# Batched inverses in smaller bundles, another accumulator bank for a transposing stage, and an undivided last tile

## The chip, the cores and the metric

The kernel runs on one core of one Trainium2 chip. The core has a matmul engine (PE, with its weight loads PEld), a vector engine (DVE), an activation engine (ACT), a small general engine (POOL) and a queue that issues transfers (SP). The metric is the device time of one execution in microseconds; smaller is better. The kernel before was run three times: 1584.83, 1586.66 and 1587.31 us.

## The reference

One layer of a decoder on 1024 tokens of width 2048, all in float32. A normalised input is projected, three groups of heads work on the columns, and a second projection with a residual and a final norm closes it.

```python
h = rmsnorm(x, ln_g[l])
proj = h @ w_in[l]
# group A: per chunk of 128 tokens, four groups of 128 channels
out_a = gmlp_spatial_gating(g_u, g_v, ...) * silu(g_z)
# group B: 8 heads of 128, chunks of 64 tokens
a = where(strict, einsum('bhnid,bhnjd->bhnij', kb, k) * decay, 0.0)
T = triangular_solve(a + eye, eye, left_side=True, lower=True, unit_diagonal=True)
value = einsum('bhnij,bhnjd->bhnid', T, vb)
...
_, o = lax.scan(step, s0, xs)          # state from chunk to chunk
out_b = rmsnorm(o, dn_norm_g[l]) * silu(d_z)
# group C: attention into 256 memory tokens, 4 heads
out_c = softmax(scores) @ mv * silu(c_z)
x = x + concatenate([out_a, out_b, out_c]) @ w_out[l]
return rmsnorm(x, final_g)
```

The spatial gating normalises `gelu(g_v)` over its 512 channels and multiplies it, chunk by chunk, by a lower triangular 128x128 matrix per group.

## The kernel before

**Tiling.** Both projections are cut into two halves of tokens, two halves of the inner dimension and two halves of columns, and are computed with seven products of half-size blocks in place of eight (`seven`, L1289; the order of the seven is `ORDER`). Every float32 operand is split into a rounded part and a remainder (`split_to`: a cast on ACT, a subtraction on DVE), and each product is the sum of three matmuls of 128x128 by 128x512, so almost all of PE's time is 128x512 matmuls into eight accumulator banks: `acc0` to `acc3` and `dn0` to `dn3` (in the profile `acc` and `dn`). In the order listings below the numbers behind the names are those of the buffers: `dn_111` to `dn_114` are `dn0` to `dn3`, `acc_107` to `acc_110` are `acc0` to `acc3`.

**Stages.** The projection runs as `project_stage` calls: columns of the first four delta heads, of the other four, gates and values, then pairs of column blocks for groups A and C, then the output projection. The small work of the heads runs between the large matmuls: `front` (convolution, norms and the chunk matrices of a pair of heads), `inverse` and `levels` (the triangular inverses of 32 chunk matrices at once, called twice: "a" for heads 0 to 3, L1550, and "b" for heads 4 to 7, L1646), `back` (the scan over chunks), `spatial` (the normalisation of `g_v`, L1620), `attend`.

**The inverses.** `inverse` inverts the 32x32 diagonal blocks on DVE, and `levels` (L1032) joins them to 64x64 and then 128x128 blocks with small float32 products on PE, in the banks `dn0` and `dn1` (there called `da`, `db`, and `dy` for both). Each batch of these products is a bundle: inside `with R.together()` the products of one batch are put next to each other in PE's order. There are four bundles in each inverse: 64 products of 32x32, 96 of 32x32, 32 of 64x64, 32 of 64x64. Copies on ACT and DVE stand between them. The results go out to memory (`ulo`, `umid`, `uhi`, written on SP) and come back with `load_u` (L1109) as the tile `ut`, which the scan multiplies by (`dn<-vs,ut` and `dn<-steps,ut`).

**What sets the order.** Nothing is issued as it is written. Each call is recorded in a `Plan` with its dependences; `price` (L183) gives it a cost and, in `o.lat`, a latency that its readers on other engines have to wait. `lay` (L233) lays the operations on the engines by these numbers, `late` (L322) works out latest starts from the end, the two alternate for `PASSES` rounds, and `issue` emits the best plan. So all instructions have one line in the profile, L398 (`o.fn(...)`), and one changed number can move instructions anywhere. On the chip each engine works through its list in that order and waits where data are missing. SP is such a list too: a transfer that waits for its source holds all transfers behind it. `AHEAD` (L70) is how far, in nanoseconds, the plan lets SP run ahead of the transfers in flight. `behind(op)` adds a dependence on `op`; accumulator banks are tracked whole, so any write to a bank waits for every earlier read of it.

**The end.** The last tile of the output (128 tokens, 512 columns, in `dn0`) takes 12 last products; `take` adds it to the residual on DVE, `square` sums its squares on ACT, `close` (L1779) turns the sum into a scale (POOL) and scales four column blocks, which go out. Before the change the last tile is computed and added in two halves of 256 columns, one after the other, in the same bank.

## Time and profile before

| what | value |
|---|---|
| runs shown | 1584.83, 1586.66, 1587.31 us |
| profiled execution, its own time | 1587.73 us |
| its span | 1586.0 us |
| mean granted PE clock | 0.995 |
| PE busy | 1559.0 us, 98% |
| DVE busy | 1219.6 us, 77% |
| ACT busy | 931.7 us, 59% |
| transfers | 431.40 MB, mean 272 GB/s |

Times in the views are microseconds from the start of the span, unless marked ns. In a line of the timeline the first number is the start, the second the duration, `x2` a count of like instructions, and in brackets the idle time of that engine just before and what ended it. "issue" names a wait for nothing that the profile shows. A matmul's duration reaches past the start of the next one, since matmuls are pipelined. A float32 product appears as two matmul records, each with its weight load. `q8 instruction` is a transfer queue that carries instructions. A view by stretches gives, for each engine, busy time and instruction count, then the granted share of the PE clock.

### The profile page before, as it was taken

What the parts mean: (1) busy time and instruction counts of PE and PEld (TensorE: products, weight loads), DVE (VectorE), ACT (ScalarE), POOL (GpSimd) and SP (SyncE); (2) the same over time, 40 slices, a digit from 0 to 9 for tenths busy, and PEclk for the clock granted to TensorE, in tenths of its full rate; (3) what the DMA queues carried; (4) which work ended last, traced back from release to release, by engine and by line L of the source; (5) the groups of instructions that cost most, each with busy time, mean ns of one, the idle gap of its engine ahead of it and who ended that gap; (6) DMA issues with size and microseconds to landing.
All of it is one profiled execution on the core that took longest, in us unless ns stands there. A gap on an engine that the chain in (4) does not pass through costs nothing.

```text
span 1586.0 us, 25201 instructions
## 1 busy us (share of the span) xinstructions
PE 1559.0 (98%) x8773; PEld 1309.6 (83%) x8773; DVE 1219.6 (77%) x1802; ACT 931.7 (59%) x1921; POOL 102.1 (6%) x125
## 2 busy tenths in 40 slices
PE   8999999999999999999999999999999999999997
PEld 7987888888888778888888778888888888888886
DVE  6966844789979756887799667878668888688775
ACT  7832455767854247778864444876657864344455
POOL 0100001010020001110110010000000000000001
PEclk9999999999999999999999999999999999999999
DMA  9999866999988797886989896898868979678657
GB/s 328 305 333 330 288 182 201 323 324 336 301 260 275 236 294 245 263 282 193 276 275 319 240 261 218 279 343 284 257 211 267 310 263 351 214 269 294 227 151 274
DMA packets 338353, 431.40 MB, mean 272 GB/s; under 512 B 77353, under 2 KB 163890, under 8 KB 338226
## 3 DMA queue, kind: packets, MB, share of 16 engines
q1 hardware_dynamic: 336642, 427.09, 84.0%
q0 software_dynamic: 1088, 2.10, 0.4%
q8 instruction: 69, 1.13, 0.3%
q10 hardware_dynamic: 496, 0.61, 0.1%
q14 instruction: 58, 0.48, 0.1%
HBM read 330.29 MB, written 99.42 MB: 271 GB/s over the span
## 4 chain that ended last, share of the span: by engine, by line
PE 85%; DMA 4%; issue 1%; ACT 1%; DVE 1%; SPq 1%; POOLq 0%; POOL 0%; ACTq 0%; DVEq 0%
PE acc L398 53%; PE dn L398 32%; SPq L398 1%; DMA raw<-in_w_in_dram 1%; DMA E<-ed 1%; DMA late<-os 0%; DMA xr<-pd 0%; DMA kd<-late 0%; DMA ut<-uloa 0%; DMA ut<-in_x_dram 0%; DMA qT<-late 0%; DMA ll<-hsd 0%; ACT obs L398 0%; DVE tn L398 0%; ACT rhi L398 0%
## 5 line engine op out<-in xcount | busy, mean ns | idle before, releaser
L398 PE MATMUL acc<-lh,rhi 128*128 128x512 f32 x1024 | 396.6, 396 | 1.8 <-DVE obs L398 1.8
L398 PE MATMUL acc<-lh,rlo 128*128 128x512 f32 x1024 | 387.1, 396 | 0.2 <-DVE rlo L398 0.2
L398 ACT CAST rhi<-raw 128x1024 fp32r<-128x1024 f32 (+1 forms) x148 | 186.6, 1261 | 244.8 <-PE dn L398 119.3
L398 DVE TENSOR_TENSOR rlo<-raw,rhi 128x1024 fp32r<-128x1024 f32 (+1 forms) x148 | 219.3, 1482 | 106.6 <-ACT rhi L398 103.1
L398 PE MATMUL acc<-ll,rhi 128*128 128x512 f32 x688 | 269.9, 397 | 0.0
L398 PEld LDWEIGHTS acc<-lh,rhi 128*128 128x128 f32 x1024 | 193.3, 189 | 39.4 <-DVE obs L398 2.6
L398 PEld LDWEIGHTS acc<-lh,rlo 128*128 128x128 f32 x1024 | 193.0, 189 | 37.5 <-DVE rlo L398 0.7
L398 DVE TENSOR_TENSOR ll<-ll,lh 128x1024 fp32r<-128x1024 f32 x122 | 149.9, 1229 | 17.3 <-ACT lh L398 17.0
L398 PEld LDWEIGHTS acc<-ll,rhi 128*128 128x128 f32 x688 | 129.7, 189 | 24.8 <-DVE ll L398 0.2
L398 ACT CAST lh<-ll 128x1024 fp32r<-128x1024 f32 x122 | 127.9, 1048 | 23.2 <-DMA ll<-hsd 5.6
L398 PE MATMUL acc<-lm,rhi 128*128 128x512 f32 x336 | 133.4, 399 | 0.0
L398 PE MATMUL dn<-lh,rhi 128*128 128x512 f32 x288 | 112.9, 393 | 0.4 <-issue 0.4
L398 PE MATMUL dn<-lh,rlo 128*128 128x512 f32 x288 | 107.6, 393 | 0.0
L398 DVE TENSOR_TENSOR raw<-raw,kept 128x1024 f32<-128x1024 f32 (+1 forms) x56 | 81.1, 1452 | 3.6 <-DMA raw<-in_w_in_dram 3.6
L398 PE MATMUL dn<-ll,rhi 128*128 128x512 f32 x192 | 75.4, 394 | 0.0
L398 PEld LDWEIGHTS acc<-lm,rhi 128*128 128x128 f32 x336 | 63.6, 189 | 12.0
L398 DVE TENSOR_TENSOR rlo<-kept,rhi 128x1024 fp32r<-128x1024 f32 (+1 forms) x29 | 41.9, 1446 | 37.2 <-ACT rhi L398 37.1
L398 ACT CAST rhi<-kept 128x1024 fp32r<-128x1024 f32 (+1 forms) x29 | 35.7, 1230 | 51.4 <-PE dn L398 25.6
L398 POOL TENSOR_TENSOR hs<-hs,mhalf 128x4 f32<-128x4 f32 x32 | 45.8, 1436 | 273.7 <-DVE hs L398 262.6
L398 PEld LDWEIGHTS dn<-lh,rhi 128*128 128x128 f32 x288 | 54.3, 188 | 10.8
L398 PEld LDWEIGHTS dn<-lh,rlo 128*128 128x128 f32 x288 | 53.9, 188 | 10.4
L398 POOL TENSOR_TENSOR small<-small,mhalf 128x1 f32<-128x1 f32 x26 | 21.3, 819 | 580.7 <-DVE small L398 580.7
(412 smaller groups left out, 3395.8 us busy)
## 6 DMA issues: line engine op xcount, KB each, us to landing
raw<-in_w_in_dram SPq DMA_DIRECT2D x120, 512.0 KB
ll<-hsd SPq DMA_DIRECT2D x54, 512.0 KB
raw<-in_w_out_dram SPq DMA_DIRECT2D x48, 512.0 KB
raw<-in_w_in_dram SPq DMA_DIRECT2D x72, 256.0 KB
lm<-hsd SPq DMA_DIRECT2D x26, 512.0 KB
pd<-obs SPq DMA_DIRECT2D x48, 256.0 KB
late<-os SPq DMA_DIRECT2D x44, 256.0 KB
kept<-in_w_in_dram SPq DMA_DIRECT2D x20, 512.0 KB
```

What stands on the lines that cost most here:

```text
L398: o.fn(*o.args, **o.kw)
```

## The change

Five things are edited.

1. In `levels` the bundles are cut to 32 products: the first into two halves over `k` with a copy of its own each, the second into three (first the products into `da`, then those into the rows `r` of `db`, then those into the rows `q`). Each bundle but the first is put `behind` the operation recorded last, a copy of an earlier result, so that bundles cannot stand next to each other in the plan. The products are the same, 224 in each inverse; there are seven bundles instead of four.
2. `price` gives every small float32 product (fewer than 128 output rows and columns, no transpose) 3500 ns more of latency (`FETCH`), which makes the plan expect its readers later.
3. `AHEAD` goes from 2000 to 1000 ns.
4. `spatial` and the transposes for its matrices use the bank `dn2` in place of `dn1`; the call of `spatial` is recorded behind the four assignments that followed it. In `heads_out` the loaded gate goes to a buffer of the ring `E` in place of `sm`.
5. The last tile is computed, added and squared in one piece of 512 columns.

```diff
-    FIRST, SPREAD, PASSES, STRETCH, AHEAD = 0, 1.75, 5, 1.0, 2000.0
+    FIRST, SPREAD, PASSES, STRETCH, AHEAD = 0, 1.75, 5, 1.0, 1000.0
+    FETCH = 3500.0
...
-            o.lat = 175.0
+            o.lat = 175.0 + (0.0 if out.shape[0] == P or n == P or name == "transpose" else self.FETCH)
...
+            for e in range(2):
+                ks = slice(8 * e, 8 * e + 8)
+                with behind(R.ops[-1] if e else R.gate), R.together():
+                    for k in range(16)[ks]:
+                        for r in range(4):
+                            t = tu[low(r), k] if r % 2 else tlo[low(r), k, low(0)]
+                            PE.matmul(da[low(r), k], gc[low(r), k], t, start=True, stop=True)
+                S.copy(yc[:, ks], da[:, ks])
+            blocks = [(k, h, low(2 * h), low(2 * h + 1)) for k in range(16) for h in range(2)]
             with R.together():
-                for k in range(16):
-                    for r in range(4):
-                        t = tu[low(r), k] if r % 2 else tlo[low(r), k, low(0)]
-                        PE.matmul(da[low(r), k], gc[low(r), k], t, start=True, stop=True)
-            S.copy(yc, da)
-            with R.together():
-                for k in range(16):
-                    for h in range(2):
-                        r, q = low(2 * h), low(2 * h + 1)
-                        PE.matmul(db[q, k], yc[r, k], tu[r, k], start=True, stop=True)
-                        PE.matmul(db[r, k], yc[q, k], uhi[q, k, low(1)], start=True, stop=True)
-                        PE.matmul(da[q, k], tu[r, k], yc[r, k], start=True, stop=True)
+                for k, h, r, q in blocks:
+                    PE.matmul(da[q, k], tu[r, k], yc[r, k], start=True, stop=True)
             for h in range(2):
                 S.copy(tlo[low(2 * h + 1), :, low(0)], da[low(2 * h + 1)])
+            with behind(R.ops[-1]), R.together():
+                for k, h, r, q in blocks:
+                    PE.matmul(db[r, k], yc[q, k], uhi[q, k, low(1)], start=True, stop=True)
+            for h in range(2):
                 V.tensor_copy(uhi[low(2 * h), :, low(1)], db[low(2 * h)])
+            sides = [(x_, h, w) for x_ in range(8) for h in range(2) for w in range(2)]
+            with behind(R.ops[-1]), R.together():
+                for k, h, r, q in blocks:
+                    PE.matmul(db[q, k], yc[r, k], tu[r, k], start=True, stop=True)
             S.copy(ux, db)
-            with R.together():
+            with behind(R.ops[-1]), R.together():
                 for x_, h, w in sides:
...
-                e, y = sums(), ob.rearrange("p t c -> p (t c)")
+                e, y = ring["E"](), ob.rearrange("p t c -> p (t c)")
...
-                    if last and key == order[-1] and t == NT - 1:
-                        for cols in (slice(0, HT // 2), slice(HT // 2, HT)):
-                            for h in held:
-                                product(t, *h, cols=cols)
-                            takes[key](t, bank[t], cols)
-                        return
                     for h in held:
                         product(t, *h)
...
-            bank = dnr.bufs[1]
+            bank = dnr.bufs[2]
```

What the plan makes of it, at three places. The whole order of PE, DVE, ACT and SP is laid anew, so rows differ everywhere; the instructions themselves stay the same but for the last tile (12 matmuls of 512 columns for 24 of 256, and one addition, one square and one small sum fewer) and the loads of ACT's function tables, of which the list holds 27 in place of 19. Nine of the 27 stand at the attention (from the first to the last exponential of `attend`), where three stood.

PE at the first inverse, before: the end of the first bundle (64 products into `dn0`), four large matmuls, the start of the second (96 products).

```order
L398 MATMUL dn_111<-gt_434,inv_432 32x32
L398 MATMUL dn_111<-inv_432 32x32
L398 MATMUL acc_110<-lh,rhi_76 128x512
L398 MATMUL acc_107<-lh,rhi_77 128x512
L398 MATMUL acc_107<-ll,rhi_77 128x512
L398 MATMUL acc_107<-lh,rlo_75 128x512
L398 MATMUL dn_112<-inv_432,inv_433 32x32
L398 MATMUL dn_112<-gt_435,inv_433 32x32
L398 MATMUL dn_111<-inv_433,inv_432 32x32
```

PE at the same inverse, now: the third bundle (32 products, one row) between large matmuls.

```order
L399 MATMUL dn_114<-lh,rhi_77 128x512
L399 MATMUL dn_114<-ll,rhi_77 128x512
L399 MATMUL dn_111<-inv_433,inv_432 32x32 x32
L399 MATMUL acc_107<-lh,rlo_75 128x512
L399 MATMUL acc_108<-lh,rlo_75 128x512
L399 MATMUL acc_109<-lh,rlo_75 128x512
L399 MATMUL acc_110<-lh,rlo_75 128x512
```

Before, the four bundles of an inverse have 4, 8 and 4 large matmuls between them; now the seven bundles of the first have 22, 18, 19, 22, 19 and 20.

SP behind the last bundle of the first inverse, before: `umida` is written, and `ut_82` is what the first scan reads (`kept`, `raw` and `ll` are operands of the large matmuls, `pd` a result).

```order
L398 DMA pd_5_160<-obs 128x512
L398 DMA umida<-gt_434 64x16x64 x2
L398 DMA ut_82<-uloa 32x8x32
L398 DMA ll<-h0d 128x2x512
L398 DMA kept_80<-in_w_in_dram 128x2x512
L398 DMA ut_82<-uhia 64x8x64
L398 DMA kept_80<-in_w_in_dram 128x2x256
L398 DMA raw_72<-in_w_in_dram 128x2x512
L398 DMA ut_82<-umida 64x8x64
```

SP at the same place, now.

```order
L399 DMA ut_83<-uhia 64x8x64
L399 DMA raw_73<-in_w_in_dram 128x2x512
L399 DMA umida<-gt_434 64x16x64
L399 DMA raw_73<-in_w_in_dram 128x2x256
L399 DMA ll<-h0d 128x2x512
L399 DMA umida<-gt_434 64x16x64
L399 DMA raw_72<-in_w_in_dram 128x2x512
L399 DMA ut_82<-umida 64x8x64
```

The other parts of `ut` are loaded ahead of `umida`, and one operand load instead of four stands between its last write and its load. On PE, between the last bundle of the first inverse and the first scan product that reads `ut`, 57 large matmuls and 8 transposes stood; now there are 74 and 8. Behind the second inverse there were 434 large matmuls, 44 transposes and 20 other float32 products; now there are 61, 16 and 8.

DVE at the end, before: `kd_515` is the last tile, added in two pieces, `small_103` and `small_104` are the sums of squares of the last two tiles.

```order
L398 TENSOR_TENSOR kd_515<-dn_111,kd_515 128x256
L398 SCALAR_TENSOR_TENSOR small_103<-small_103 128x1
L398 SCALAR_TENSOR_TENSOR small_104<-small_104 128x1
L398 SCALAR_TENSOR_TENSOR kd_514<-kd_514,small_103,fg_501 128x512
L398 TENSOR_SCALAR qT_510<-qT_510,small_103 128x512
L398 TENSOR_TENSOR kd_515<-dn_111,kd_515 128x256
```

DVE at the end, now.

```order
L399 SCALAR_TENSOR_TENSOR small_103<-small_103 128x1
L399 SCALAR_TENSOR_TENSOR kd_514<-kd_514,small_103,fg_501 128x512
L399 TENSOR_TENSOR kd_515<-dn_111,kd_515 128x512
L399 TENSOR_SCALAR qT_510<-qT_510,small_103 128x512
L399 SCALAR_TENSOR_TENSOR small_104<-small_104 128x1
```

The one addition stands behind one scaling of the tile before, where the second half stood behind two.

More of the change, by code (lines that the diff above doesn't have):

```diff
@@ L1085, in levels @@
+            for h in range(2):
                 V.tensor_copy(uhi[low(2 * h), :, low(1)], db[low(2 * h)])
+            sides = [(x_, h, w) for x_ in range(8) for h in range(2) for w in range(2)]
+            with behind(R.ops[-1]), R.together():
+                for k, h, r, q in blocks:
+                    PE.matmul(db[q, k], yc[r, k], tu[r, k], start=True, stop=True)
             S.copy(ux, db)
-            sides = [(x_, h, w) for x_ in range(8) for h in range(2) for w in range(2)]
-            with R.together():
+            with behind(R.ops[-1]), R.together():
@@ L1294, in seven, with product @@
             bank = banks(key)
-            def product(t, i, a, ws, part=None, cols=None):
+            def product(t, i, a, ws, part=None):
                 for u in range(2):
@@ L1302, in product @@
                         r = [x_[:, u * HT : (u + 1) * HT] for x_ in (hi, lo)]
-                        if cols:
-                            r, o = [x_[:, cols] for x_ in r], o[:, cols]
                     else:
@@ L1661 @@
         V.scalar_tensor_tensor(bt[g], tp[:, sl], col2[:, 4 + g : 5 + g], bsb[:, sl], op0=ALU.mult, op1=ALU.add)
-    for hf in range(2):
-        spatial(hf)
     scan_banks = dnr.bufs[0:2]
@@ L1667 @@
     el = over([abh[:, 0:HT], ring["tn"].bufs.pop()])
+    for hf in range(2):
+        spatial(hf)
     with rank(2.6):
@@ L1796, in close, with square @@
             to.dma_start(out[r0 : r0 + P, c * HT : (c + 1) * HT], y)
-    def square(half_, t, c, cols=slice(0, HT)):
-        S.activation(jk[:, cols], ys[half_][t][c][:, cols], AF.Square, accum_out=ssy[half_][t][:, c : c + 1])
+    def square(half_, t, c):
+        S.activation(jk, ys[half_][t][c], AF.Square, accum_out=ssy[half_][t][:, c : c + 1])
     oh = halves(own(os, "oh", "alo1", 4 * HT))
@@ L1846, in final, with take @@
             put = more(m, key, after)
-            def take(t, a, cols=slice(0, HT)):
-                r = ssy[key[0]][t]
-                if cols.stop - cols.start < HT:
-                    add(y[key][t][:, cols], a[:, cols], y[key][t][:, cols])
-                    square(key[0], t, c, cols)
-                    total(r) if cols.start == 0 else close(key[0], t)
-                    return
+            def take(t, a):
                 put(t, a)
                 square(key[0], t, c)
+                r = ssy[key[0]][t]
                 if c == 3:
```

8 lines of the change are left out of this document (3 added, 5 removed).

## The prediction

> **What bounds the kernel now.** I read the page first: busy time, the chain that ended last, the queues.
>
> ```profile
> span 1586.0 us, 25201 instructions
> PE 1559.0 (98%) x8773; PEld 1309.6 (83%) x8773; DVE 1219.6 (77%) x1802; ACT 931.7 (59%) x1921; POOL 102.1 (6%) x125
> PE 85%; DMA 4%; issue 1%; ACT 1%; DVE 1%; SPq 1%; POOLq 0%; POOL 0%; ACTq 0%; DVEq 0%
> ```
>
> PE is the bound nearly everywhere, so only what PE does not do while it could counts. Next the view by stretches: a dense one, the two inverses, the three pieces of them in which the clock is low, and the attention.
>
> ```profile
> core 0: us, PE busy (x) PEld busy (x) DVE busy (x) ACT busy (x) POOL busy (x), PEclk, DMA share, GB/s
> 545.00:590.00 45.00, 40.57 (x597) 32.56 (x596) 20.62 (x26) 18.33 (x34) 1.06 (x2) 0.92 0.95 262
> 556.20:559.60 3.40, 3.40 (x9) 2.44 (x8) 2.06 (x3) 1.74 (x3) 0.00 (x0) 0.50 1.05 343
> 580.10:583.50 3.40, 2.94 (x9) 2.58 (x10) 1.00 (x2) 0.96 (x3) 0.10 (x1) 0.50 1.17 261
> 895.00:930.00 35.00, 28.91 (x545) 22.62 (x544) 18.34 (x27) 13.21 (x18) 4.01 (x5) 0.95 0.91 248
> 904.40:907.80 3.40, 3.40 (x8) 2.10 (x7) 2.60 (x3) 1.61 (x3) 0.00 (x0) 0.51 0.87 255
> 1180.00:1280.00 100.00, 100.00 (x515) 84.32 (x514) 85.45 (x143) 76.68 (x175) 3.34 (x2) 1.00 0.85 278
> 1420.00:1560.00 140.00, 140.00 (x619) 115.97 (x618) 112.69 (x143) 68.07 (x97) 2.28 (x3) 1.00 0.68 227
> ```
>
> The last row gives the price of a large matmul: 140 us for 619 is 0.226 us. The inverses are where PE loses time: 45.00 - 40.57 = 4.43 us idle in the first, 35.00 - 28.91 = 6.09 us in the second, and three stretches of 3.4 us at half the clock, in which 9, 9 and 8 matmuls start where 15 would. PE's own waits say for what:
>
> ```profile
> PE dn L398 <- issue: 5.8, 5, 2.4
> PE dn L398 <- DMA ut<-uloa: 2.7, 1, 2.7
> PE acc L398 <- DVE obs L398: 1.8, 1, 1.8
> ```
>
> The last two lie in the two stretches, and so does the first, but for 0.1 us: 1.5 in the first stretch and 4.2 in the second (first two rows below). I ask next whether these "issue" waits belong to the instruction supply.
>
> ```profile
> PE dn L398 <- issue: 1.5, 2, 1.1
> PE dn L398 <- issue: 4.2, 3, 2.4
> 554.84 0.21 PE L398 MATMUL dn<-gt,inv 32*32 32x32 f32 x1 [1.09 <-issue]
> 902.76 0.21 PE L398 MATMUL dn<-inv,inv 32*32 32x32 f32 x1 [2.40 <-issue]
> q8 instruction: 69, 1.13, 0.3%
> q8 instruction: 4, 0.07, 1.1%
> ```
>
> The longest of each stand in the middle of the 96 products of the second bundle, where no data are awaited. The queue q8 carries 69 packets in the run (fifth row) for 2 x 8773 PE instructions, about 254 to a packet, and 4 of them in the 25 us from 545 to 570 (last row), where an even share would be one. The first two bundles are 160 products, 640 instructions, two and a half packets within 6 us. So I take the pauses for packets that come too late.
>
> **The change, part by part.**
>
> *Bundles.* 32 products are 128 instructions, half a packet, and 18 to 22 large matmuls (4.1 to 5.0 us at 0.226) follow, with some 40 instructions more. A packet then lasts over 7 us instead of some 2, and the issue waits go: 10.52 us of idle time hold 5.7 of them. What a bundle's border costs I read at the first one.
>
> ```profile
> 550.02 0.39 PE L398 MATMUL acc<-lh,rlo 128*128 128x512 f32 x1
> 550.34 0.21 PE L398 MATMUL dn<-gt,inv 32*32 32x32 f32 x1
> 551.44 0.19 PE L398 MATMUL dn<-inv 32*32 32x32 f32 x1
> 551.56 0.73 PE L398 MATMUL acc<-lh,rhi 128*128 128x512 f32 x2
> 552.13 0.39 PE L398 MATMUL acc<-ll,rhi 128*128 128x512 f32 x1
> ```
>
> From the large matmul to the first small one 0.32 us pass instead of 0.23, from the last small one to a large one 0.12, where small ones follow each other every 0.017, and the next two large ones take 0.57 instead of 0.45: 0.09 + 0.10 + 0.12 = 0.31 us. Six bundles more make 1.9 us lost. That is the one sure loss. The Trainium skill's page "TensorEngine Tiling (Array Packing)", section "Key Properties", speaks against the edit here: a change of tiling mode (full array to 32x32 tiles and back) drains the engine, so more bundles mean more drains. The trace agrees, the 0.31 us being such borders; by the page, which prices none, the sum would have the same sign there.
>
> *Latency in the plan.* The real stalls made the bundles late against the plan, and what was due behind them arrived late too: `ut` at the first scan, and `obs` at 928.9 us, whose weights stood on SP behind the writes of the second inverse's results. With 3.5 us per bundle in the plan (the measured pauses being 1.09 and 2.40) I expect these waits to be planned for. The chain from the last bundle to the first scan is the place to test it.
>
> ```profile
> 562.21 0.94 PE L398 MATMUL dn<-gt,inv 64*64 64x64 f32 x52
> 563.24 0.59 ACT L398 COPY gt<-dn 128x512 f32<-128x512 f32 x1 [1.68 <-DMA kept<-in_w_in_dram]
> 567.68 1.30 SPq L398 DMA_DIRECT2D umida<-gt  x2
> 573.18 0.61 SPq L398 DMA_DIRECT2D ut<-umida  x1
> 580.56 1.19 PE L398 MATMUL dn<-vs,ut 128*128 128x128 f32 x4 [2.70 <-DMA ut<-uloa]
> ```
>
> From 563.15, the bundle's end, to 580.56 are 17.4 us: 0.7 to the copies' end, then 3.8 in which SP is held by `pd` and other transfers, 5.5 from the write's issue to the load's, 7.4 to the scan. PE has work between: 57 large matmuls, 12.9 us, and 8 transposes before; now 74, 16.7 us, and 8 small ones, between 0 and 8 x 0.226 = 1.8. So 16.7 to 18.5 us against 17.4, with fewer transfers between: a wait of at most 0.7. Behind the second inverse stand 61 large ones, 13.8 us, and 24 small ones, 0 to 5.4, together 13.8 to 19.2, where there were 434: the same chain there can wait between 0 and 3.6 us. I take 2.0, the middle, which is near the two waits of 1.8 and 2.7.
>
> *AHEAD.* Loads stand up to 1 us later in the plan. Between 0 and one more wait like that for `obs` (1.8 us, and 1.5 for a stretch at half clock behind it). The plan before left hardly any wait outside the inverses and the start, in some 1500 us; I take 0 and keep 3.3 for the range.
>
> *The clock.* All three stretches at half clock follow a wait (554.84, 580.56, 902.76). Without long waits PE keeps its clock: 6 x 0.226 = 1.4 us, (3.40 - 0.46) / 2 = 1.5 (part of that stretch is idle and counted above), 7 x 0.226 = 1.6: 4.5 us come back. From below: 0, if bundles of 0.6 us pull it down themselves; the first bundle (64 products, 1.1 us) didn't.
>
> *Bank and ring.* `spatial` on `dn2` frees it from the second inverse's banks, which is what lets its transposes and the first scans move up beside that inverse. No instruction is added; eight loads get another buffer. What hides them is PE's large matmuls; if that cover went, it would be the 3.6 us above. Taken at 0, with the price in the wait there.
>
> *The last tile.*
>
> ```profile
> 1574.04 0.69 DVE L398 TENSOR_TENSOR kd<-dn,kd 128x512 f32<-128x512 f32 x1 [0.72 <-PE dn L398]
> 1574.83 0.63 ACT L398 ACTIVATE jk<-kd 128x512 bf16<-128x512 f32 x1
> 1576.18 0.39 PE L398 MATMUL dn<-oh 128*128 128x256 f32 x1 [0.74 <-DVE kd L398]
> 1577.59 0.28 PE L398 MATMUL dn<-rhi,fl 128*128 128x256 f32 x1
> 1577.91 0.42 DVE L398 TENSOR_TENSOR kd<-dn,kd 128x256 f32<-128x256 f32 x1
> 1578.72 0.42 ACT L398 ACTIVATE jk<-kd 128x256 bf16<-128x256 f32 x1 [0.53 <-DVE kd L398]
> ```
>
> The second half waits 0.74 us for the addition of the first, as both are in one bank. Twelve halves take 1577.59 - 1576.18 + 0.12 = 1.5 us, so both 3.0 and the wait 3.7; twelve matmuls of 512 take 12 x 0.226 = 2.7, 1.0 less. The addition takes 0.69 instead of 0.42, the square 0.63 instead of 0.42: 0.5 more. Net 0.5 us earlier; the bounds are 1.0 earlier, if DVE gets to it at once, and 0.5 later, if PE's gain is lost behind the scaling on DVE.
>
> *Sum.* 10.5 idle, and 1.4 more because the view takes a matmul's end late (928.94 has 1.84 us idle before it, but starts 2.24 us after the matmul at 926.70, which is 2.01 over the 0.23 it needs; 0.17 for each of the eight waits), and 4.5 of clock: 16.4 us to gain. Less 1.9 of borders and 2.0 of waiting for `ut`, plus 0.5 at the end: 13.0.
>
> ```profile
> 926.70 0.39 PE L398 MATMUL acc<-lh,rlo 128*128 128x512 f32 x1
> 928.94 0.50 PE L398 MATMUL acc<-lh,rhi 128*128 128x512 f32 x1 [1.84 <-DVE obs L398]
> ```
>
> The profiled execution took 1587.73 us (span 1586.0), the median of the runs is 1586.66, 0.07% less; I take the gain from the median: 1573.7.
>
> **The rivals.**
>
> *Slower: ACT's tables at the attention.* ACT loads 27 tables instead of 19, nine instead of three at the attention.
>
> ```profile
> L398 ACT ACT_TABLE_LOAD x3 | 3.8, 1283 | 0.4 <-DVE small L398 0.3
> ```
>
> One takes 1.283 us. If each of the six more delays a cast on which PE waits, and each wait brings a stretch at half clock (1.5), it is 6 x 2.8 = 16.8 us, and the result 1586.7 - 13.0 + 16.8 = 1590.5. It turns the gain from five such waits on. For it: ACT is busy for 76.68 of 100 us there, and 7.7 more make 84. Against it: PE is busy for 100.00 of 100 there with three loads inside, so casts have lead.
>
> *The waits for transfers stay.* If `ut` (2.7) and the late weights (1.8) wait as before, with one half-clock stretch (1.5) and 0.3 for their ends, 6.3 us come back less, though the 2.0 is then counted already: 13.0 - 4.3 = 8.7, or 1578.0. For it: SP is in order, and 13.8 to 19.2 us against 17.4 is tight. Against it: fewer transfers stand in the chain.
>
> *The bundle gets smaller and the pauses stay.* If the "issue" waits come from the small products and not from late packets, 5.7 us, five ends (0.8) and two stretches (3.0) stay: 13.0 - 9.5 = 3.5, or 1583.2. For it: the waits stand only inside and just behind bundles. Against it: the first bundle, 64 products, had none, and q8's four packets in 25 us. A page of the Trainium skill says what would give this: "Runtime: NRT & Kernel Launch", section "Instruction fetch mechanics", has instructions fetched in blocks of 256 with the fetch hidden, since dispatch is slower than the refill. The block agrees with the 254 here; that it is hidden does not agree with the 1.09 and 2.40 us.
>
> **How the numbers follow.** The forecast 0.58; the waits for transfers stay 0.20; the pauses stay 0.06; nothing to be told from no change 0.04; slower, by the tables or by loads that AHEAD makes late in many places, 0.12. About 0.2% (3.2 us) is what a measurement of this kernel can tell from no change. Faster 0.84, same 0.04, slower 0.12. The forecast alone lies between 1571.2 (no wait for `ut`, 1.0 at the end) and 1578.6 (3.6 for `ut` and 3.3 for AHEAD). Below, the range takes in 3 us of slow starts near the waits that no row counts as idle; above, it reaches on to the pauses that stay: 1568 to 1584.
>
> **What would show it.** PE's waits: "issue" under 1 us, no packet-late pause inside a bundle, the wait for `ut` under 3.6. The clock: 1.00 through both inverses. The records: bundles of 32 products in about 0.6 us with 18 and more large matmuls between. The end: twelve last matmuls without a break, the last square at about 1.2 us behind their end. Wrong would be: PE idle by more than 5 us in all behind the start, ACT waited for at the attention, or the half clock back at the bundles.

## The result, and the profile after

The changed kernel takes 1579.44 us (median of five runs, 1575.45 to 1581.35), the kernel before, run beside it, 1587.19 (1584.83 to 1589.31). The ratio is 0.9952 with a 95% interval of 0.9933 to 0.9970: 7.8 us gained, by the interval between 4.8 and 10.6. The forecast of 1573.7 was 5.7 us too low, and its gain of 13.0 us lies outside the interval; the range held the time.

The profiled execution of the changed kernel took 1581.31 us (before 1587.73). First its page, then PE's waits behind the first 160 us, without one for `os` (0.4) and one for a load (0.2), then four stretches of the changed kernel and, last, one of before (PE busy and count, the same for PEld, DVE, ACT, POOL, then the granted clock, the share of the DMA engines and GB/s).

```profile
span 1579.3 us, 25145 instructions
PE 1558.6 (99%) x8761; PEld 1306.8 (83%) x8761; DVE 1219.1 (77%) x1800; ACT 941.2 (60%) x1929; POOL 98.5 (6%) x125
```

```profile
PE dn L399 <- ACT steps L399: 1.3, 1, 1.3
PE acc L399 <- DVE lm L399: 0.8, 1, 0.8
PE dn L399 <- ACT xa L399: 0.7, 1, 0.7
PE dn L399 <- ACT inv L399: 0.6, 1, 0.6
PE acc L399 <- DVE ll L399: 0.3, 1, 0.3
PE dn L399 <- ACT E L399: 0.3, 1, 0.3
```

```profile
560.00:620.00 60.00, 60.00 (x681) 48.68 (x680) 32.26 (x29) 25.51 (x37) 1.05 (x2) 1.00 0.84 234
935.00:980.00 45.00, 44.35 (x618) 35.98 (x617) 26.80 (x32) 18.42 (x25) 4.40 (x6) 1.00 0.82 217
1000.00:1020.00 20.00, 17.47 (x96) 14.13 (x96) 15.18 (x26) 11.98 (x25) 2.13 (x3) 1.00 1.03 318
1240.00:1252.00 12.00, 11.09 (x57) 8.90 (x56) 9.06 (x17) 9.29 (x20) 0.00 (x0) 1.00 0.95 315
1000.00:1020.00 20.00, 20.00 (x95) 16.52 (x94) 17.32 (x23) 19.03 (x26) 0.86 (x2) 1.00 0.94 305
```

No wait is put down to "issue" any more, and none to `ut`. The first two rows of the last fence are the two inverses, which now stand a little later: PE is idle for 0 and 0.65 us in them (4.43 and 6.09 before), at the full clock. The third and fourth row are new losses: 2.53 us idle beside the scans of the second four heads, 0.91 us at the attention, where before had none (last row; at the attention 100.00 of 100 in the row that the prediction shows). In the second inverse 15 to 22 large matmuls stand between the bundles, fewer at two places than the 18 that the prediction named.

A second account takes PE's starts instead of its busy time, since a busy PE need not be at its peak. From each start to the next I take off what that kind of instruction needs in undisturbed work (a large matmul 0.227 us, a small product of 32x32 0.018, of 64x64 0.030, the other kinds likewise) and add up what is left over, by stretch. "After again" is the profile of the same changed kernel from a later group of runs (e9 below, span 1577.1 us).

| stretch, us | before | after | after again |
|---|---|---|---|
| 540–620, first inverse | 10.2 | 3.7 | 3.7 |
| 620–880, first scans, gates | 3.1 | 4.0 | 4.3 |
| 880–980, second inverse | 10.7 | 4.8 | 5.2 |
| 980–1020, second scans | 0.2 | 4.5 | 1.8 |
| 1220–1300, attention | 0.7 | 2.1 | 2.8 |
| from 1540, the end | 0.9 | 0.0 | 0.0 |
| all else | 12.8 | 12.6 | 11.6 |
| sum | 38.6 | 31.7 | 29.4 |

The inverses give back 12.4 us, nearly what the prediction had for them (16.4 of idle time and clock, less 1.9 for borders and 2.0 for `ut`: 12.5). Then 4.3, 0.9 and 1.4 us more than before are lost at the second scans, the first scans and the attention, 6.6 us in all. The last column shows how firm these are: the same kernel lost 2.7 us less at the second scans in another execution, and 0.7 more at the attention, 4.9 us in all. The stretch of the second scans doesn't hold the same work in both kernels: the first scan product behind the second inverse starts at 1024.1 us before, and at 995.5 now.

*What is left in the inverses.* PE in the changed kernel, at the third bundle of the first inverse (`x64` counts two records for each of 32 products):

```profile
578.53 0.39 PE L399 MATMUL dn<-ll,rhi 128*128 128x512 f32 x1
578.85 1.20 PE L399 MATMUL dn<-inv,inv 32*32 32x32 f32 x64
579.98 1.20 PE L399 MATMUL acc<-lh,rlo 128*128 128x512 f32 x4
```

From the last large matmul to the first small product 0.32 us, as before. But from the first small product to the next large matmul it is 1.13 us, of which 0.13 is the border: 1.00 us for 32 products, 0.032 each. The bundles of the first stage take 0.55 us for the same number, 0.017 each. Those go round all four groups of 32 rows; the three bundles into which the second stage is cut use only two of the four at a time. Six such bundles cost 6 x 0.45 = 2.7 us more than the price of 0.017 says.

*The scan behind the second inverse* starts without a wait, 0.23 us behind the matmul ahead of it:

```profile
995.27 0.39 PE L399 MATMUL acc<-lh,rhi 128*128 128x512 f32 x1
995.50 0.60 PE L399 MATMUL dn<-vs,ut 128*128 128x128 f32 x4
```

*The second scans.* The waits there, ACT's rows first, then PE's:

```profile
1009.41 1.05 ACT L399 CAST lh<-lm 128x1024 fp32r<-128x1024 f32 x1 [4.07 <-DMA lm<-hsd]
1011.95 1.28 ACT L399 ACT_TABLE_LOAD   x1 [1.49 <-DMA vd<-sm]
1013.24 0.60 ACT L399 ACTIVATE sm<-dn 128x512 f32<-128x512 f32 x1
1013.74 0.44 ACT L399 ACTIVATE steps<-dn 128x128 f32<-128x128 f32 x2
```

```profile
1011.78 0.50 PE L399 MATMUL acc<-lm,rhi 128*128 128x512 f32 x1 [0.76 <-DVE lm L399]
1014.06 0.71 PE L399 MATMUL dn<-steps,kd 128*128 128x128 f32 x4 [1.32 <-ACT steps L399]
```

ACT works through its list in order. A cast waited 4.07 us for its load, then a table load stood for 1.49 us until a transfer out of the buffer of `spatial` (`vd<-sm`) was done, took 1.28 us itself, and `spatial`'s 0.60 us followed; the scan's `steps` stood behind all of it, and PE waited for them.

*The attention.* ACT's cast of `xa`, for which PE waits, and the cast ahead of it:

```profile
1248.93 1.05 ACT L399 CAST rhi<-raw 128x1024 fp32r<-128x1024 f32 x1 [1.11 <-DMA raw<-in_w_out_dram]
1249.89 0.36 ACT L399 CAST xa<-dn 128x256 fp32r<-128x256 f32 x1
1250.30 0.50 PE L399 MATMUL dn<-xa,inv 128*128 128x512 f32 x1 [0.66 <-ACT xa L399]
```

A cast that waited 1.11 us for its load held `xa` up. In e9's profile it waited 2.17 us, and PE 1.71. No table load stands between 1195 us and this place; the next one is behind `xa`, at 1250.54.

*The end.* The additions and squares of the last two tiles, and the scaling:

```profile
1567.70 0.69 DVE L399 TENSOR_TENSOR kd<-dn,kd 128x512 f32<-128x512 f32 x1 [0.94 <-PE dn L399]
1570.85 0.68 DVE L399 TENSOR_TENSOR kd<-dn,kd 128x512 f32<-128x512 f32 x1
1571.62 0.63 ACT L399 ACTIVATE jk<-kd 128x512 bf16<-128x512 f32 x1
1573.20 0.75 DVE L399 SCALAR_TENSOR_TENSOR kd<-kd,small,fg 128x512 f32<-128x512 f32 x1 [0.66 <-POOL small L399]
```

From the addition of the last tile but one to the first scaling of the last one are 5.50 us; before it was 6.05 (1574.04 to 1580.09). So the end is 0.55 us shorter.

### The profile page after: what moved, and what is told of

Same layout as the page of the kernel before. It is cut to its first block, busy times and chain, and to the rows that moved or that the text cites. A ratio compares the mean times of both kernels' runs of the same rounds, so it can differ in the third digit from the quotient of the medians.

```text
span 1579.3 us, 25145 instructions
## 1 busy us (share of the span) xinstructions
PE 1558.6 (99%) x8761; PEld 1306.8 (83%) x8761; DVE 1219.1 (77%) x1800; ACT 941.2 (60%) x1929; POOL 98.5 (6%) x125
## 3 DMA queue, kind: packets, MB, share of 16 engines
q8 instruction: 69, 1.13, 0.3%
## 4 chain that ended last, share of the span: by engine, by line
PE 93%; DMA 4%; ACT 1%; SPq 1%; issue 1%; DVE 1%; POOLq 0%; POOL 0%; ACTq 0%; DVEq 0%
PE acc L399 56%; PE dn L399 37%; DMA raw<-in_w_in_dram 1%; SPq L399 1%; DMA ll<-hsd 1%; DMA raw<-in_w_out_dram 1%; DMA ut<-umida 0%; ACT rhi L399 0%; DMA vd<-sm 0%; DMA sq<-xd 0%; DVE rlo L399 0%; DMA kept<-in_mem_dram 0%; DMA ggd<-gt 0%; ACT os L399 0%; ACT L399 0%
## 5 line engine op out<-in xcount | busy, mean ns | idle before, releaser
L399 POOL TENSOR_TENSOR hs<-hs,mhalf 128x4 f32<-128x4 f32 x32 | 42.6, 1333 | 280.6 <-DVE hs L399 270.9
```

What stands on the lines that cost most here:

```text
L399: o.fn(*o.args, **o.kw)
```

## The experiments

All ratios are against the kernel before, run on the same chip beside them. Three groups of runs: e1 to e4 (before 1584.69 us), e5 to e8 (1585.52), e9 to e12 (1585.33).

**e1: the bundles alone.** Before, with edits 1 and 2 (smaller bundles, apart, and the latency of 3500 ns). The old bank, the old `AHEAD` and the old end stay.

```diff
 # against the changed kernel
-    FIRST, SPREAD, PASSES, STRETCH, AHEAD = 0, 1.75, 5, 1.0, 1000.0
+    FIRST, SPREAD, PASSES, STRETCH, AHEAD = 0, 1.75, 5, 1.0, 2000.0
...
-            bank = dnr.bufs[2]
+            bank = dnr.bufs[1]
```

> The kernel before with the two edits of the inverses alone: seven bundles of at most 32 products that lie apart, and 3500 ns more latency for small products in the plan. The old bank, the old lead of the load queue (2000 ns) and the last tile in two halves stay. Theory (late instruction packets and the half clock behind them were the loss): no wait by 'issue' inside a bundle, clock 1.00 through both inverses, PE without a wait in the first inverse, and the time 7 to 10 us under the kernel before, so at least what the whole change gained (7.75 us). Rival (the gain came from the other edits): less than 3 us gained.

Measured: 1588.31 us, ratio 1.0016 [1.0005, 1.0028], slower than before, where a gain of 7 to 10 us was expected. No wait is left at the bundles, but for one of 1.9 us for a cast between those of the second inverse. The large loss is new and stands in front of the first inverse, where the small work of the heads (`front`) runs. A stretch of e1, the same of before (second row), and PE's longest waits in it in e1:

```profile
370.00:420.00 50.00, 42.59 (x197) 34.09 (x197) 45.49 (x91) 40.95 (x134) 2.65 (x5) 0.90 0.96 323
370.00:420.00 50.00, 50.00 (x262) 42.33 (x261) 48.10 (x88) 44.11 (x135) 1.52 (x3) 1.00 0.96 319
```

```profile
PE dn L399 <- ACT kd L399: 2.5, 2, 2.1
PE acc L399 <- ACT rhi L399: 2.4, 1, 2.4
PE dn L399 <- ACT kT L399: 1.0, 1, 1.0
```

7.4 us idle and a clock of 0.90; before had no idle time there. DVE is busy for 45.49 of 50 us and ACT for 40.95, and PE waits for them. The bundles do what the prediction said of them, and the plan that comes with them loses it all again in front of them.

**e2: the other three edits alone.** The changed kernel with the old bundles and no latency for them (edits 3, 4 and 5 stay).

```diff
-            o.lat = 175.0 + (0.0 if out.shape[0] == P or n == P or name == "transpose" else self.FETCH)
+            o.lat = 175.0
...
+            with R.together():
+                for k in range(16):
+                    for r in range(4):
+                        t = tu[low(r), k] if r % 2 else tlo[low(r), k, low(0)]
+                        PE.matmul(da[low(r), k], gc[low(r), k], t, start=True, stop=True)
+            S.copy(yc, da)
...
```

> The other edits alone: lead of the load queue 1000 ns, the bank dn2 and the ring E for the gating, the last tile in one piece; bundles of 64, 96, 32 and 32 and the old latency. Theory: the pauses inside the second bundles (1 us and more each) and the half clock stay, the end is 0.5 to 1 us shorter, new waits beside the scans cost 0 to 3 us: between 1 us faster and 3 us slower than before. Rival (these edits carry the gain): at least 5 us faster.

Measured: 1583.74 us, 0.9995 [0.9984, 1.0007], no difference, as the theory expected. The pauses stay, at 7.6 us even longer than before, with half the clock around the longest (0.91 over the first inverse):

```profile
PE dn L398 <- issue: 7.6, 4, 4.5
```

```profile
560.00:600.00 40.00, 35.46 (x568) 28.91 (x567) 16.79 (x17) 12.87 (x15) 0.96 (x1) 0.91 0.87 232
```

**e3: the latency alone.** Before, with `FETCH` (edit 2) and nothing else; the old bundles of 64 and 96.

```diff
+    FETCH = 3500.0
-            o.lat = 175.0
+            o.lat = 175.0 + (0.0 if out.shape[0] == P or n == P or name == "transpose" else self.FETCH)
```

> The kernel before with the 3500 ns of latency alone; bundles as before. Theory: the plan leaves room behind each bundle, so the waits for the first scan's operand (2.7 us) and for late weights (1.8 us) go, but pauses of 1 to 2.5 us inside the bundles of 96 stay, as they come from the products' own supply, with a stretch at half clock behind each: 3 to 7 us faster. Rival (the plan's times alone were wrong): as fast as the whole change, with no 'issue' wait inside a bundle.

Measured: 1582.9 us, 0.9984 [0.9969, 0.9999]: 2.5 us, just told from none and under the 3 to 7 expected. The pauses stay; telling the plan of them does not make them go, and `ut` is waited for at one place still:

```profile
PE dn L399 <- issue: 4.9, 2, 3.3
PE dn L399 <- DMA ut<-umida: 1.7, 1, 1.7
```

Besides, 3.6 us are lost at 360 to 440 us, by PE's starts; the table under e6 comes back to that.

**e4: mixed bundles in the second stage.** The changed kernel, but the products into `da` and those into the rows `r` of `db` are cut by `k` into two mixed bundles of 32, which together use all four groups of rows; the copies are cut likewise.

```diff
-            with R.together():
-                for k, h, r, q in blocks:
-                    PE.matmul(da[q, k], tu[r, k], yc[r, k], start=True, stop=True)
...
+            for e in range(2):
+                ks = slice(8 * e, 8 * e + 8)
+                with behind(R.ops[-1]), R.together():
+                    for k, h, r, q in blocks[16 * e : 16 * e + 16]:
+                        PE.matmul(da[q, k], tu[r, k], yc[r, k], start=True, stop=True)
+                        PE.matmul(db[r, k], yc[q, k], uhi[q, k, low(1)], start=True, stop=True)
...
```

> The changed kernel, but the second stage of the inverse in two bundles that mix products from both row groups of a pair (even to odd, odd to even) and one that doesn't, with the copies halved too. In the changed kernel's trace 32 products that use four row groups take 0.55 us from first to last, 32 that use two take 1.00. Theory (products in the same two row groups follow each other at half the rate): the four mixed bundles take about 0.6 us instead of 1.00, 1.6 to 1.8 us less in all; in the timing 0 to 3 us faster than the changed kernel. Rival (the rate depends on which stage it is, its copies or its bank): still 1.00 us.

Measured: 1577.03 us, 0.9958 [0.9943, 0.9972]. PE at a mixed bundle (its first product, the last, and the large matmul behind it):

```profile
580.87 0.21 PE L399 MATMUL dn<-inv,inv 32*32 32x32 f32 x1
...
581.43 0.19 PE L399 MATMUL dn<-gt,inv 32*32 32x32 f32 x1
581.55 0.50 PE L399 MATMUL acc<-ll,rhi 128*128 128x512 f32 x1
```

0.56 us from first to last, where the unmixed bundle takes 1.00, and the other three mixed bundles take 0.55 to 0.59. So the rate goes with the number of groups of rows that a bundle uses (those that it reads and those that it writes grow together here), and the 2.7 us of the changed kernel are a matter of how the 96 products were cut. The four bundles save 1.8 us; the time, against that of the changed kernel, cannot show so little: its five runs lie 5.9 us apart.

**e5: AHEAD back to 2000.** The changed kernel with edit 3 undone.

```diff
-    FIRST, SPREAD, PASSES, STRETCH, AHEAD = 0, 1.75, 5, 1.0, 1000.0
+    FIRST, SPREAD, PASSES, STRETCH, AHEAD = 0, 1.75, 5, 1.0, 2000.0
```

> The changed kernel with the load queue's lead put back to 2000 ns. The kernel with the two edits of the inverses alone lost about 14 us between 380 and 420 us of its trace, where heads 4 to 7 aren't begun and the first fronts run; its inverses were clean. Theory A (the lead decides how the plan packs the fronts): the waits on ACT and DVE at 380 to 420 us come back, 5 to 14 us, and the time is that of the kernel before or above, 1584 to 1592 us. Theory B (any new order may fall badly there, by chance of the plan): no such waits, 1575 to 1582 us.

Measured: 1581.51 us, 0.9966 [0.9954, 0.9978]. That overlaps with both measurements of the changed kernel, so edit 3 has no effect that these runs can tell. The profiled execution is the slowest of its seven (1585.37 us) and shows one long wait, at the first scan behind the second inverse, with half the clock around its end (0.91 over 40 us); the fronts are clean, unlike those of e1:

```profile
1004.03 1.19 PE L399 MATMUL dn<-vs,ut 128*128 128x128 f32 x4 [4.73 <-issue]
```

```profile
985.00:1025.00 40.00, 35.22 (x186) 29.83 (x185) 29.90 (x48) 26.49 (x52) 1.85 (x3) 0.91 0.97 295
380.00:420.00 40.00, 40.00 (x205) 33.77 (x204) 37.95 (x61) 31.19 (x87) 2.84 (x2) 1.00 0.94 313
```

The profile names no releaser for it. The last pieces of `ut` were issued on SP at 997.05 and 999.35, 7.0 and 4.7 us earlier, and no packet of q8 begins in the 14 us ahead of the wait's end, so I take it for these loads; that is argued, not shown.

**e6: the bank back.** The changed kernel with edit 4 undone.

```diff
-            bank = dnr.bufs[2]
+            bank = dnr.bufs[1]
...
-                e, y = ring["E"](), ob.rearrange("p t c -> p (t c)")
+                e, y = sums(), ob.rearrange("p t c -> p (t c)")
...
```

> The changed kernel with the gating's transposes back on dn1, its call in the old place and the gate's buffer in the old ring. Theory A (the lead is what keeps the fronts clean; the bank lets the gating run into the scans): fronts clean, the waits for ACT and DVE at 1005 to 1014 us of the changed kernel's trace (about 3 us) gone, 1574 to 1580 us. Rival (the bank is what the change needs): waits of 5 us or more at the fronts or behind the second inverse, 1582 us or more.

Measured: 1584.21 us, 0.9993 [0.9984, 1.0002]. Without the edit that I had costed at nothing, nothing of the gain is left. Not because of `spatial`, though: the second scans run better here than in the changed kernel (second row below, 0.06 us idle in 80 us). The loss is in the fronts again, as in e1, 6.4 us idle at a clock of 0.92:

```profile
375.00:420.00 45.00, 38.58 (x194) 32.03 (x193) 41.66 (x86) 36.75 (x119) 1.16 (x3) 0.92 0.92 312
940.00:1020.00 80.00, 79.94 (x386) 66.66 (x385) 61.30 (x81) 46.26 (x66) 3.89 (x7) 1.00 0.79 249
```

What e1 and e6 have in common, with e3 and e10 (below) beside them, can be counted in PE's list: how many large matmuls stand ahead of the first inverse.

| kernel | large matmuls ahead of the first inverse | loss at 360–440 us, by PE's starts | ratio |
|---|---|---|---|
| before | 1988 | 0.6 | |
| changed | 2066 | 0.4 | 0.9952, 0.9964 |
| e1 | 1784 | 14.1 | 1.0016 |
| e6 | 1830 | 11.0 | 0.9993 |
| e3 | 1927 | 3.6 | 0.9984 |
| e10 | 1974 | 1.7 | 1.0001 |

160 to 200 large matmuls less than before, in e6 and e1, are 36 to 45 us less for the small work of four heads, whose chunk matrices the inverse needs. All four and before itself have the old bank, e3 and before have the old bundles too, and the loss falls in step as the inverse moves back: it goes with the place, and neither the bank nor the bundles by themselves make it. DVE had little to spare there before (57.67 us busy between 370 and 430). e10 tests this.

**e7: one bundle of 96.** The changed kernel, but the second stage is one bundle of 96 products again, still apart from the others.

```diff
-            with R.together():
+            with behind(R.ops[-1]), R.together():
                 for k, h, r, q in blocks:
+                    PE.matmul(db[q, k], yc[r, k], tu[r, k], start=True, stop=True)
+                    PE.matmul(db[r, k], yc[q, k], uhi[q, k, low(1)], start=True, stop=True)
                     PE.matmul(da[q, k], tu[r, k], yc[r, k], start=True, stop=True)
...
```

> The changed kernel with the second stage of the inverse in one bundle of 96 products again, but apart from its neighbours. Theory (PE holds what is left of one packet of instructions and one more; the next is asked for when a packet is begun and serves 2.4 to 2.7 us later): with 20 large matmuls ahead, a bundle of 96 (384 instructions, one and a half packets, 2 us) pauses 0 to 1.3 us, by where in it a packet ends, less than the 1.27 and 2.6 us of before. Rival (the size of a bundle alone makes the pause): pauses of 1 us and more in both inverses.

Measured: 1588.52 us in one run. The pauses are back, longer than the theory's 1.3 us at most, one in the bundle of 96 of each inverse and nowhere else; PE's longest waits in the two stretches, and the row behind the first of them:

```profile
PE dn L399 <- issue: 4.1, 1, 4.1
PE dn L399 <- issue: 3.8, 1, 3.8
591.95 0.26 PE L399 MATMUL dn<-inv,inv 32*32 32x32 f32 x2 [4.12 <-issue]
```

A packet of q8 begins at 583.70, before the bundle starts at 585.50; 95 products run, which is 380 instructions; PE is dry from 587.8; the next packet begins only at 589.67, and PE goes on 2.28 us later. In the second inverse the packets begin at 956.25 and 962.76 and PE goes on at 964.98, 2.22 us later. So a bundle that is half as large again as a packet (384 instructions to about 254) outruns the supply by itself. The two neighbouring bundles of before were not needed for it.

**e8: the end alone.** Before with edit 5.

```diff
-                    if last and key == order[-1] and t == NT - 1:
-                        for cols in (slice(0, HT // 2), slice(HT // 2, HT)):
-                            for h in held:
-                                product(t, *h, cols=cols)
-                            takes[key](t, bank[t], cols)
-                        return
```

> The kernel before with the last tile in one piece and nothing else. Theory: from the first of the last tile's closing matmuls to the end of the span 0.5 to 1 us less than before, no wait of PE between halves; pauses and half clock in the inverses as before; the single time 1583 to 1589 us. Rival (the order laid anew moves other work too): other stretches differ by over 2 us.

Measured: 1586.95 us in one run; a term this small is read from the trace, at the same two points as above:

```profile
1573.17 0.69 DVE L398 TENSOR_TENSOR kd<-dn,kd 128x512 f32<-128x512 f32 x1 [0.71 <-PE dn L398]
1578.68 0.75 DVE L398 SCALAR_TENSOR_TENSOR kd<-kd,small,fg 128x512 f32<-128x512 f32 x1 [0.66 <-POOL small L398]
```

5.51 us, against 6.05 before and 5.50 in the changed kernel: 0.54 us are the end's own. No stretch of the table of the result differs from before by 2 us, which would have spoken for the rival.

**e9: the changed kernel again.** No edit.

> The changed kernel again, beside the kernels of this group, as their measure. From its five runs so far (0.9952 [0.9933, 0.997]) I expect 0.995 to 0.997 of the time of before, near 1579.

Measured: 1578.48 us, 0.9964 [0.9952, 0.9977]. It came out as expected. PE's waits are of another length than in the first profile, `xa` 1.7 us for 0.7 and `lm` 0.6 for 0.8:

```profile
PE dn L399 <- ACT xa L399: 1.7, 1, 1.7
PE acc L399 <- DVE lm L399: 0.6, 1, 0.6
```

**e10: the old bank with a smaller latency.** e6 with `FETCH` 1000.

```diff
-    FETCH = 3500.0
+    FETCH = 1000.0
```

> The changed kernel with edit 4 undone (as in e6) and FETCH 1000 in place of 3500. In the plan the first inverse now stands behind 1974 large matmuls (1830 in e6, 1988 before, 2066 after), with 7 to 14 large matmuls between its bundles in place of 18 to 22. Theory of the place: what e6 and e1 lost at 375 to 420 us comes from the first inverse standing 160 to 200 large matmuls (36 to 45 us) earlier, so that the heads' small work in front of it is pressed into less time; then the loss there falls from 10 us to under 2 and the time to 1576 to 1580 (0.994 to 0.9965). Rival, the bank: with dn1 for the gate's transposes the small work is in the way wherever the inverse stands; the loss stays and the time is 1583 to 1586 (0.998 to 1.000).

Measured: 1585.19 us, 1.0001 [0.9988, 1.0013]. The first inverse stands behind 1974 large matmuls, and the loss in the fronts is gone (1.7 us at 360 to 440), though the bank is the old one and DVE is as busy as ever:

```profile
375.00:420.00 45.00, 45.00 (x239) 38.23 (x237) 43.25 (x81) 38.66 (x115) 1.01 (x1) 1.00 0.96 317
```

So the loss goes with the place of the first inverse. But the time is not better. In the profiled execution 5.3 us are lost at the first scan, behind a first inverse whose bundles stand closer together; the profile names no releaser here either, and no packet of q8 begins in the 14 us ahead of its end:

```profile
588.85 1.19 PE L399 MATMUL dn<-vs,ut 128*128 128x128 f32 x4 [5.29 <-issue]
```

In the second inverse PE pauses for 0.69 us inside a bundle of 32 products, 2.75 us behind the start of a packet at its end: with 7 to 14 large matmuls between, the supply is not always in time. Both expectations fall in part: the mechanism of the first was right and its time wrong, the time of the second was right and its mechanism wrong.

**e11: no latency in the plan.** The changed kernel with `FETCH` 0: the same bundles, 3 to 9 large matmuls apart.

```diff
-    FETCH = 3500.0
+    FETCH = 0.0
```

> The changed kernel with FETCH 0: the same seven bundles of 32 products, but only 3 to 9 large matmuls (0.7 to 2 us) between them in place of 18 to 22. Theory of the supply: 128 instructions every 1.6 to 3 us use up a packet of 256 in some 3 to 5 us, while PE resumed 2.3 to 2.7 us after a packet began and that began up to 2 us late; pauses of 1 us and more come back in one or both inverses, with half the clock behind them: 3 to 6 us lost, time 1581 to 1585 (0.997 to 1.000). Rival, the size of the single bundle decides (64 products never paused inside, 96 nearly always): no pause above 0.5 us, half clock nowhere, 1576 to 1580 (0.994 to 0.9965).

Measured: 1583.34 us, 0.9987 [0.9975, 0.9999], by the two ratios 3.6 us worse than the changed kernel beside it (0.9964). A pause is back inside a bundle of 32 products of 64x64:

```profile
581.68 0.47 PE L399 MATMUL dn<-gt,ut 64*64 64x64 f32 x17 [1.29 <-issue]
```

A packet begins at 579.37, and PE goes on 2.3 us later. So the supply theory held in the pause and in the time, but no half clock came back in this execution. The profiled execution is the fastest of the ten (1579.07 us); what the others lost on top, no trace shows. The distance between small bundles matters, though less than the size of a single one (the pauses of e7 are 4.1 and 3.8 us).

**e12: e4 with FETCH 1000.**

> e4 (second stage in mixed bundles) with FETCH 1000: 8 to 13 large matmuls (1.8 to 2.9 us) between the bundles in place of 16 to 22, and the plan laid anew. Theory of the supply: 128 instructions and some 20 to 30 more in 2.5 to 3.8 us are near what it can follow, pauses under 1 us in all; mixed bundles take 0.55 us in place of 1.00; 1574 to 1578 (0.9925 to 0.9955), at or under e4. Rival, more lead in the plan is what keeps the results in time: with less of it PE waits longer for copies and for ut behind the bundles (3 us and more), 1579 to 1582 (0.996 to 0.998).

Measured: 1578.33 us, 0.9961 [0.9947, 0.9976], not to be told from the changed kernel (0.9964 beside it) or from e4, and just above the range that was expected. No gap inside a bundle of 32x32 products is over 0.13 us; PE waits for copies between them instead (`gt`, 1.8 us in two waits). Behind the longer of them, 1.1 us, half the clock is back once (0.91 over 940 to 960 us).

## Why the prediction was right in direction and too high in size

- **The pauses.** Right. "A packet then lasts over 7 us instead of some 2, and the issue waits go": they are gone in the changed kernel and come back with the bundle of 96 (e7), with the old bundles (e2, e3), and in part with too little between the bundles (e10, e11). The rival that smaller bundles keep their pauses fell. One point of the reasoning was off: the 160 products of two bundles within 6 us were not needed, one bundle of 96 does it. The Trainium skill, page "Runtime: NRT & Kernel Launch", section "Instruction fetch mechanics", has blocks of 256 instructions and a fetch that is mostly hidden. The 69 packets for 2 x 8761 PE instructions, about 254 each, agree with the first; the pauses of 4.1 and 3.8 us in e7 do not agree with the second.
- **The clock.** Right: 1.00 through both inverses.
- **The borders.** Right in size (0.32 us to the first small product, 0.13 behind the last).
- **The products.** Wrong: "small ones follow each other every 0.017" was read from the first bundle and used for all. Those of the second stage, unmixed, take 0.032: 2.7 us that the sum did not have. Mixed ones (e4) take 0.018.
- **The wait for `ut`.** "I take 2.0" did not occur in the changed kernel. So it is in part luck that the inverses gave back what was forecast: this term, which wasn't needed, stood in for the 2.7 us of the slower products. The upper bound of 3.6 was too low for plans like this one, if the waits of 4.7 and 5.3 us at such a scan in e5 and e10, the same kernel but for one or two edits, are for `ut` (argued, not shown).
- **AHEAD.** Taken at 0; e5 tells no difference, and can't exclude one of 1 or 2 us.
- **Bank and ring.** "Taken at 0" was the wrong price, in two ways. The first is where part of the forecast's surplus went (4.3 us at the second scans, 1.6 in e9's profile). As the prediction says, the edit "lets its transposes and the first scans move up beside that inverse", and there time is lost: in the six kernels with the old bank (before, e1, e3, e6, e8, e10) the first scan behind the second inverse starts at 1018.7 to 1026.2 us, behind the last transposes of `spatial`, and by PE's starts at most 0.6 us are lost at 980 to 1020; in the seven with the new bank it starts at 968 to 1004 us, ahead of them, and 0.9 to 8.2 us are lost there. ACT's rows above show how: `steps` stood behind the work of `spatial`. The second is the plan as a whole, which I didn't ask about. With the smaller bundles, `FETCH` 3500 and the old bank the plan puts the first inverse 36 to 45 us earlier and starves PE in the fronts (e1, e6): without this edit the bundles bring nothing. Of the six timings with bundles of 32 and the new bank (the changed kernel twice, e4, e5, e11, e12) five lie between 0.9952 and 0.9966 and one at 0.9987; the three with the old bank (e1, e6, e10) lie between 0.9993 and 1.0016. Why the plan answers so to the bank stays open. That the early inverse costs the time is supported by e3 and e10, where the loss shrank as it moved back, and not proved, since the plan changed elsewhere too.
- **The rest of the sum.** This is the step that failed most: under *AHEAD* the prediction took it that "the plan before left hardly any wait outside the inverses" and gave the new plan the same. It lost 6.6 us more than before (4.9 in e9's profile) at the first scans and gates, the second scans and the attention; the rows above for the last two show PE waiting for work of ACT and DVE that stood behind loads. The sum with what was measured: 16.4 - 1.9 - 2.7 + 0.5 - 6.6 = 5.7, against 6.7 between the two spans; 1 us of the inverses' gain is not placed.
- **The tables.** ACT was waited for at the attention (`xa` 0.7 and 1.7, `E` 0.3), which the prediction named as a sign of being wrong, but not because of its tables: the casts stood behind loads, and no table load was ahead of them. So the rival's mechanism did not show there. Beside the scans a table load of 1.28 us did lengthen a chain for which PE waited (at 1011.95); before has one ahead of `spatial` too, at 1003.51, without a wait of PE.
- **The end.** Right: 0.5 forecast, 0.55 measured, 0.54 alone (e8).

## What to carry to other kernels

A run of very short instructions has to be counted in instructions, not in time: here 32 small products (128 instructions) with 3.4 us and more of long work behind them never paused, and all ten bundles of 96 in one piece (384) did, for 1.1 to 4.5 us (before, e2, e3, e7, e8). When a planner lays the order, an edit's price is not what the edit moves but what the whole new plan does: look first at where each large stage now stands, count the long instructions ahead of it, and ask whether the work that feeds it still has its time. Of the 12.4 us that came back at one place here, 6.6 were lost at others, so a gain at one place of a tight schedule is not yet a gain of the kernel.

## What was not expected of the hardware

- The rate of small products depends on how many groups of rows a bundle goes round: 0.017 to 0.018 us each with four, 0.032 with two, for the same 32x32 product (e4 and the changed kernel).
- After a pause PE goes on 2.2 to 2.8 us behind the start of a packet of instructions (2.75 and 2.43 before, 2.28 and 2.22 in e7, 2.31 in e11), and that packet can itself begin 1.6 to 1.8 us after PE has run dry (e7).
- The same program takes 1575.45 to 1581.35 us from run to run at a clock of 0.998 to 0.999, and its waits behind loads and casts change by 1 us and more between two profiles of it. With runs that far apart, an effect under 3 us needs more than five of them, or has to be read from the trace at its own place.
